# A seventh raw weight tile, and the second tile split first, in an f32 encoder layer on one core

## The chip, the cores and the metric

The kernel runs on 1 core of one Trainium2 chip. The metric is the device time of one execution in microseconds, the median of several runs. The core's engines are TensorE (PE in the profile; PEld is its weight load), VectorE (DVE), ScalarE (ACT), GpSimd (POOL) and SyncE (SP), which issues most DMAs.

## The reference

One pre-norm residual layer over x (256 tokens x 2048 channels, float32), then a final RMSNorm:

```python
h = _rms_norm(x, norm_g)
proj = jnp.einsum('bsd,dn->bsn', h, w_in)        # q k v o za | gates | xb zb | ga gb
ya = _mlstm_branch(q_p, k_p, v_p, o_p, za_p, gif_p, b_if, head_g)
yb = _rglru_branch(xb_p, zb_p, conv_w, conv_b, w_rg, b_rg, lam)
ya = jnp.einsum('bsw,wd->bsd', ya, w_branch_a)
yb = jnp.einsum('bsw,wd->bsd', yb, w_branch_b)
merged = sigmoid(ga_p) * ya + sigmoid(gb_p) * yb
return x + jnp.einsum('bsd,de->bse', merged, w_out)
```

The projections and the three output matrices are matrix products with K = 2048. They are nearly all of the arithmetic, and each weight is read from HBM once.

## The kernel before

Each matrix product is made with split operands, so that the float32 result keeps its precision: a tile v becomes `hi` (a rounded copy, made by ScalarE) and `lo` = v - hi (a subtraction on VectorE), and a product is three matmuls, a.hi + a.lo + b.hi, where a and b are the halves of the activations (`mm`, L174 to L177). A matmul has 128 x 128 weights and 512 columns.

Weights come as tiles of 128 x 1024 f32 (two K-blocks of 128 by 512 output columns, 512 KB) into six tiles of one tag, `raw`. SyncE issues these loads in program order, and each waits until a raw tile is free, that is, until the last instruction that read the load before in it has ended. Four pairs of tiles `whi`/`wlo` hold the halves.

Weights are used in two ways, both in `pair` (L163), which makes two blocks of 512 output columns at a time:

- `plain` (with `load_chunk`, L122 to L142): one raw tile, one copy (L140), one subtraction (L141), then 4 products, 12 matmuls.
- `products` (L186 to L227), called a group in this document: two raw tiles r1 (L190) and r2 (L191) are combined in Strassen's manner, so that 7 products (21 matmuls) do the work of 8. The two tiles are packed on the host so that halves can be subtracted. VectorE forms four sums of half a tile each, t1 (L199, L200) and t2 (L203, L204); four splits are made (`split`, L180 on ScalarE and L181 on VectorE): half of r1 into `b` (512 columns), t1 into h1/l1, t2 into h2/l2, and all of r2 into h3/l3. The order of the program is: b, two sums, split of t1, two sums, split of t2, split of r2. The products p1, p5, p7, p6 go to four small accumulators `aux`, the other three to the large ones, `acc`, in the order p1 (b), p5 and p7 (h1), p6 and one more (h2), and two (h3).

Which of the eight K pieces of a pair are groups, and at which places they stand, is a list by hand. In the four stages `wb` (branch b), gate b, gate a and `wa` (branch a) there are two pairs each: the first with groups at places 0, 2, 4, 6, the second at 1, 3, 5 (`S_WB` to `L_WA`). In `wo` a pair has groups at 0, 2, 4, 6; in the projections for v, o and z there are one or two groups in a pair. After the last group, `aux` is folded into the output by VectorE (L252 to L256), and at the end of a block the large accumulator is added (L262).

The order of instructions on each engine is not the program's. The build places them by a timeline model, with priorities: loads, splits and sums stand in `urgent()` blocks, where earlier program text comes first. The order is then fixed, and each engine takes its instructions one after the other. So in the trace products of a group and plain products are mixed, and a group's `b` can stand on TensorE ahead of products of the group before.

Two other places are touched. `load_chunk` and `products` take their raw tiles from the pool directly (L124, L189). Eight small tiles of 48 columns (`cat` to `spl`, L450), used for the gates near the start (`g_nat`, `g_cum`), lie in the pool of constants; other scratch of that time, the masks among it, lies in a region called E (`et`), which later becomes `hs`, the output of the recurrence.

Of the kernel before, what the change touches and what calls it, by code (L numbers as in the profile page):

```python
# [9 lines left out]
F32 = mybir.dt.float32  # L10
# [5 lines left out]
P = 128  # L16
# [3 lines left out]
NB = 512  # L20
KC = 2
# [8 lines left out]
S_WO = (0, 1, 2, 4)  # L30
L_WB, L_GB, L_GA, L_WA = [((0, 2, 4, 6), (1, 3, 5))] * 4
L_WO = (0, 2, 4, 6)
H_FORMS = (4, 0)
PLAN = (dict(Y=('c0', '', '', 'c1',),
             V=('', '', 'c2 c3', 'g0', '', '', 'g1', '', '', '', 'g2 g3',),
# [11 lines left out]
def f(ap):  # L47
    return ap.bitcast(F32)
# [3 lines left out]
def hybrid_encoder(ctx: ExitStack, tc: tile.TileContext, x, xt, pk, bif, fg, wg, wi, wr, wa, wb, wo, out):  # L52
    nc = tc.nc
    pe, act, dve, pool, sp = nc.tensor, nc.scalar, nc.vector, nc.gpsimd, nc.sync
# [3 lines left out]
    wp = ctx.enter_context(tc.tile_pool(name="wp", bufs=1))  # L58
# [6 lines left out]
    def name(n):  # L65
        uid[0] += 1
        return f"{n}_{uid[0]}"

    def ct(shape, n, dt=F32):
        return cst.tile(shape, dt, tag=n, name=n)  # L70

    def sl(tag, dt=F32, cols=4096):
        return slot.tile([P, cols], dt, tag=tag, name=name("s" + tag))
# [13 lines left out]
    def urgent():  # L87
        uid[0] += 1
        return tc.high_priority(offset=HP - 30 * uid[0])
# [28 lines left out]
        lanes.clear()  # L118

    first_dma = [None]  # L120

    def load_chunk(src, dst=None, tag="w", bufs=4, parts=1, between=()):  # L122
        with urgent():
            raw = wp.tile([P, KC * NB], F32, tag="raw", name=name("raw"), bufs=6)  # L124
            if dst is None:
                hi = wp.tile([P, KC * NB], F32R, tag=tag + "hi", name=name(tag + "hi"), bufs=bufs)
                lo = wp.tile([P, KC * NB], F32R, tag=tag + "lo", name=name(tag + "lo"), bufs=bufs)
            else:
                hi, lo = dst
            w = KC * NB // parts  # L130
            for i in range(parts):
                r = slice(i * w, (i + 1) * w)
                last_dma[0] = (act if between and i == 0 else sp).dma_start(raw[:, r], src[:, r]).ins
                if i == 0:
                    first_dma[0] = last_dma[0]
            for i in range(parts):
                r = slice(i * w, (i + 1) * w)
                if i < len(between):
                    between[i]()
                last_copy[0] = act.copy(hi[:, r], raw[:, r]).ins  # L140
                last_sub[0] = dve.tensor_sub(lo[:, r], raw[:, r], f(hi[:, r])).ins  # L141
        return hi, lo  # L142
# [17 lines left out]
    def four(v):  # L160
        return v.rearrange("p (a b) -> p a b", b=S)

    def pair(src, xhi, xlo, forms, kqs, dst, b11, epilogue, sums=None, places=None, calm=False):  # L163
        aps = []
        accs = [acc_pair()[1] for _ in range(2)]
        banks = [[v[:, :NB], v[:, NB:]] for v in accs]
# [6 lines left out]
        def mm(ps, a, b, wh, wl, stop):  # L173
            pe.matmul(ps, a, wh, start=id(ps) not in began, stop=False)  # L174
            began.add(id(ps))
            pe.matmul(ps, a, wl, start=False, stop=False)  # L176
            pe.matmul(ps, b, wh, start=False, stop=stop)  # L177

        def split(hi, lo, v):
            act.copy(hi, v)  # L180
            dve.tensor_sub(lo, v, f(hi))  # L181

        def wpair():
            return [wp.tile([P, KC * NB], F32R, tag=t, name=name(t), bufs=4) for t in ("whi", "wlo")]

        def products(kq, last):  # L186
            lf, rt_ = slice(0, NB), slice(NB, 2 * NB)
            with urgent():
                r1, r2 = [wp.tile([P, KC * NB], F32, tag="raw", name=name("raw"), bufs=6) for _ in range(2)]  # L189
                sp.dma_start(r1, src[0][kq])  # L190
                sp.dma_start(r2, src[1][kq])  # L191
                bh, bl = b11()
                split(bh, bl, r1[:, lf])
                if sums:
                    t1, t2 = sums()
                else:
                    t1, t2 = [four(hp.tile([P, 2 * NB], F32, tag=t, name=name("t"))) for t in ("vhi", "vlo")]
                v1, v2 = four(r1), four(r2)
                dve.tensor_sub(t1[:, :2], v1[:, 2:], v1[:, :2])  # L199
                dve.tensor_sub(t1[:, 2:], v2[:, :2], v1[:, 2:])  # L200
                h1, l1 = wpair()
                split(four(h1), four(l1), t1)
                dve.tensor_add(t2[:, :2], t1[:, 2:], v1[:, :2])  # L203
                dve.tensor_sub(t2[:, 2:], v2[:, 2:], t2[:, :2])  # L204
                h2, l2 = wpair()
                split(four(h2), four(l2), t2)
                h3, l3 = wpair()
                split(h3, l3, r2)
            fm = forms[kq]

            def xb(kk, tb):
                o = (kq * KC + kk) * S + tb * P
                return xhi(o, o + P), xlo(o, o + P)

            def sf(i):
                return [v[:, i * P:(i + 1) * P] for v in fm]

            if not aps:
                aps.extend(aux(i) for i in range(4))
            p1, p5, p7, p6 = aps  # L220
            mm(p1, *xb(0, 0), bh, bl, last)
            mm(p5, *sf(0), h1[:, lf], l1[:, lf], last)
            mm(p7, *sf(2), h1[:, rt_], l1[:, rt_], last)
            mm(p6, *sf(1), h2[:, lf], l2[:, lf], last)
            mm(banks[0][1], *xb(1, 1), h2[:, rt_], l2[:, rt_], False)
            mm(banks[0][0], *xb(1, 0), h3[:, rt_], l3[:, rt_], False)
            mm(banks[1][0], *sf(3), h3[:, lf], l3[:, lf], False)  # L227

        def plain(kq, jj):
            hi, lo = load_chunk(src[jj][kq])  # L230
# [170 lines left out]
    def et(shape):  # L401
        n = int(np.prod(shape[1:]))
        o = eoff[0]
        eoff[0] += n
        v = est[:shape[0], o:o + n]
        if len(shape) == 3:
            v = v.rearrange("p (a b) -> p a b", b=shape[2])
        return v
# [38 lines left out]
        pool.memset(t, 0.0)  # L447
    gn = ct([P, 2, 16], "gn")
    NS = 48
    cat, ab, ey, sv, qv, pv, ng, spl = (ct([P, NS], n) for n in ("cat", "ab", "ey", "sv", "qv", "pv", "ng", "spl"))  # L450
    c8, c4 = ct([P, 32], "c8"), ct([P, 32], "c4")
    an = et([P, 2, P])
    negM, em = ct([P, 2, 8], "negM"), ct([P, 2, 8], "em")
# [352 lines left out]
    def values(h):  # L806
        if h == 0:
            yas["h"], yas["l"] = sl("A", F32R), sl("B", F32R)
            hf.update({kq: halves(sl(f"F{kq}", F32R, 1024), 0) for kq in H_FORMS})
            for i, kq in enumerate(H_FORMS):  # L810
                rg["work"][f"y{i}"] = lambda kq=kq: forms_h(kq)
# [124 lines left out]
    def b11():  # L936
        nb11[0] += 1
        v = hp.tile([P, 2 * NB], F32R, tag=("to", "zz")[nb11[0] % 2], name=name("b11"))
        return v[:, :NB], v[:, NB:]
# [17 lines left out]
    for p in range(2):  # L957
# [5 lines left out]
        pair((wi[BLK_GA + 2 * p], wi[BLK_GA + 2 * p + 1]), hhi, hlo, forms("h"), S_GA[p], ga[2 * p:], b11, epi_ga, None, L_GA[p])  # L963
    for kq, slot_ in zip(k_ya[2:], H_FORMS[::-1]):
        fslot["a", kq] = halves(sl(f"F{slot_}", F32R, 1024), 0)
# [64 lines left out]

    pair((wo[0], wo[1]), mh, ml, mf_, S_WO, dst, b11, epi_wo, None, L_WO)

# [7 lines left out]
    for tb, a, b, col in ((0, 0, NB, 3), (1, 0, S, 3), (1, S, NB, 4)):  # L1040
        ps = aux()[:, :b - a]
        for k in range(KT):
# [4 lines left out]
            xa, xb = mh(o, o + P), ml(o, o + P)  # L1047
# [79 lines left out]
```

## Time and profile before

| | |
|---|---|
| median of 3 runs | 1028.58 us (1027.71 to 1029.91) |
| the profiled execution, its own time | 1029.06 us |
| its span, first to last instruction | 1027.3 us |
| mean granted TensorE clock | 0.995 |
| instructions | 13760 |
| raw weight loads by SyncE | 358, nearly all of 512 KB |
| HBM read | 196.33 MB, 193 GB/s over the span |

The 358 loads are the rows "raw<-wi" (254), "raw<-wb", "raw<-wa" and "raw<-wo" (32 each) and "raw<-wr" (8) of the profile's last part. Times are in microseconds from the first instruction unless marked ns. A line such as "PE aux L174 <- ACT b L180: 7.6, 4, 3.3" says that TensorE, before writing `aux` at line 174, waited for ScalarE writing `b` at line 180, 7.6 us in total, 4 times, 3.3 us at the longest. In a timeline a row has start, length, engine, line, operation, output and inputs, how many were merged, and in brackets the idle time before it and what ended it. Matmuls overlap in the records (0.39 us long): the distance of two starts is what one costs.

### The profile page before, as it was taken

How to read it: one execution, taken by the hardware profiler on the slowest of the kernel's cores; microseconds unless marked ns; L12 is line 12 of the kernel's file. 1: busy time of each engine (PE TensorE's matmuls, PEld its weight loads, DVE VectorE, ACT ScalarE, POOL GpSimd, SP SyncE). 2: the span in 40 equal slices, each digit the busy share in tenths (PEclk: the TensorE clock that was granted, in tenths of full speed). 3: DMA queues.
4: the chain of work that ended last, by engine and by line, in shares of the span. 5: the costliest groups of instructions: out<-in, count | busy, mean ns of one | idle time of the engine just before them, and what ended most of it. 6: DMA issues, size and time to landing. Idle time of an engine off the chain costs nothing.

```text
span 1027.3 us, 13760 instructions
## 1 busy us (share of the span) xinstructions
PE 1009.0 (98%) x5033; PEld 852.2 (83%) x5033; DVE 896.8 (87%) x1208; ACT 633.6 (62%) x836; POOL 19.5 (2%) x37
## 2 busy tenths in 40 slices
PE   9999999999999999999999998998999999999997
PEld 9888988888888888888888886877888788778886
DVE  6787898889769879996786898999998989999996
ACT  7546477757795776677755554545655556454562
POOL 1000000001001000100100000000000000000000
PEclk9999999999999999999999999999999999999999
DMA  9665555565665566656476465556555565567562
GB/s 349 255 207 167 160 160 190 182 204 166 197 192 164 188 198 194 198 166 212 134 227 189 156 204 187 181 166 228 183 182 207 185 205 207 175 241 282 178 209 82
DMA packets 56387, 199.32 MB, mean 194 GB/s; under 512 B 6400, under 2 KB 7424, under 8 KB 55936
## 3 DMA queue, kind: packets, MB, share of 16 engines
q1 hardware_dynamic: 55456, 197.13, 58.0%
q10 hardware_dynamic: 864, 1.32, 0.4%
q8 instruction: 39, 0.64, 0.3%
q14 instruction: 28, 0.23, 0.1%
HBM read 196.33 MB, written 2.10 MB: 193 GB/s over the span
## 4 chain that ended last, share of the span: by engine, by line
PE 79%; DVE 10%; DMA 6%; issue 3%; ACT 2%; ACTq 0%; DVEq 0%; SPq 0%
PE acc L315 16%; PE acc L176 12%; PE acc L174 12%; PE acc L177 12%; PE acc L318 8%; DMA raw<-wi 4%; DVE wlo L141 3%; PE aux L176 2%; PE aux L174 2%; PE aux L177 2%; DVE wlo L181 2%; DMA raw<-wb 1%; ACT whi L140 1%; PE aux L855 1%; PE aux L721 1%
## 5 line engine op out<-in xcount | busy, mean ns | idle before, releaser
L141 DVE TENSOR_TENSOR wlo<-raw,whi 128x1024 fp32r<-128x1024 f32 (+1 forms) x276 | 332.4, 1212 | 71.8 <-ACT whi L140 70.2
L140 ACT CAST whi<-raw 128x1024 fp32r<-128x1024 f32 (+1 forms) x276 | 285.1, 1045 | 164.5 <-PE acc L177 75.0
L176 PE MATMUL acc<-wlo,sHL 128*128 128x512 f32 x542 | 211.9, 391 | 0.0
L177 PE MATMUL acc<-whi,sHL 128*128 128x512 f32 x542 | 211.2, 390 | 0.0
L174 PE MATMUL acc<-whi,sHL 128*128 128x512 f32 x542 | 208.2, 390 | 0.0
L315 PE MATMUL acc<-sHL,whi 128*128 128x512 f32 x704 | 175.9, 393 | 0.0
L315 PEld LDWEIGHTS acc<-sHL,whi 128*128 128x128 f32 x704 | 127.4, 189 | 23.5
L180 ACT CAST whi<-t 128x1024 fp32r<-128x1024 f32 x78 | 82.0, 1052 | 65.6 <-PE acc L177 28.4
L176 PEld LDWEIGHTS acc<-wlo,sHL 128*128 128x128 f32 x542 | 101.9, 188 | 22.0 <-DVE wlo L141 0.9
L174 PEld LDWEIGHTS acc<-whi,sHL 128*128 128x128 f32 x542 | 101.9, 188 | 21.3 <-DVE xp L330 0.4
L177 PEld LDWEIGHTS acc<-whi,sHL 128*128 128x128 f32 x542 | 101.9, 188 | 20.5
L318 PEld LDWEIGHTS acc<-sHL,wlo 128*128 128x128 f32 x704 | 95.3, 190 | 6.0
L181 DVE TENSOR_TENSOR wlo<-t,whi 128x1024 fp32r<-128x1024 f32 x78 | 94.9, 1219 | 6.1 <-ACT whi L180 5.9
L318 PE MATMUL acc<-sHL,wlo 128*128 128x256 f32 x704 | 99.0, 283 | 0.0
L180 ACT CAST b<-raw 128x512 fp32r<-128x512 f32 x32 | 19.8, 621 | 62.6 <-DMA raw<-wi 33.4
L180 ACT CAST whi<-raw 128x1024 fp32r<-128x1024 f32 x41 | 43.1, 1050 | 19.9 <-PE acc L177 9.1
L181 DVE TENSOR_TENSOR wlo<-raw,whi 128x1024 fp32r<-128x1024 f32 x41 | 50.0, 1219 | 3.6 <-ACT whi L180 3.6
L199 DVE TENSOR_TENSOR t<-raw 128x512 f32<-128x512 f32 x37 | 25.4, 687 | 10.3 <-DMA raw<-wi 4.9
L176 PE MATMUL acc<-wlo,sA 128*128 128x512 f32 x86 | 33.8, 393 | 0.0
L176 PE MATMUL acc<-wlo,sC 128*128 128x512 f32 x86 | 33.8, 393 | 0.0
L177 PE MATMUL acc<-whi,sD 128*128 128x512 f32 x86 | 33.7, 392 | 0.0
L177 PE MATMUL acc<-whi,sB 128*128 128x512 f32 x86 | 33.6, 391 | 0.0
(363 smaller groups left out, 1649.7 us busy)
## 6 DMA issues: line engine op xcount, KB each, us to landing
raw<-wi SPq DMA_DIRECT2D x254, 512.0 KB, 4.1
raw<-wb SPq DMA_DIRECT2D x32, 512.0 KB, 4.2
raw<-wa SPq DMA_DIRECT2D x32, 512.0 KB, 4.3
raw<-wo SPq DMA_DIRECT2D x32, 512.0 KB, 4.6
raw<-wr SPq DMA_DIRECT2D x8, 512.0 KB, 3.9
sB<-x SPq DMA_DIRECT2D x4, 512.0 KB, 7.9
sA<-x SPq DMA_DIRECT2D x1, 2048.0 KB, 9.6
sA<-xt SPq DMA_DIRECT2D x7, 256.0 KB, 6.6
```

The source lines that it names most:

```text
L140: last_copy[0] = act.copy(hi[:, r], raw[:, r]).ins
L141: last_sub[0] = dve.tensor_sub(lo[:, r], raw[:, r], f(hi[:, r])).ins
L174: pe.matmul(ps, a, wh, start=id(ps) not in began, stop=False)
L176: pe.matmul(ps, a, wl, start=False, stop=False)
L177: pe.matmul(ps, b, wh, start=False, stop=stop)
L180: act.copy(hi, v)
L181: dve.tensor_sub(lo, v, f(hi))
L199: dve.tensor_sub(t1[:, :2], v1[:, 2:], v1[:, :2])
L315: pe.matmul(ps[m], hi[:, o:o + P], hl_t[:, 2 * k * S:2 * (k + 1) * S], start=(k == 0), stop=(turn and k == KT - 1), skip_group_check=True)
L318: pe.matmul(ps[m][:, :S], lo[:, o:o + P], hhi(k * S, (k + 1) * S), start=False, stop=(not turn and k == KT - 1), skip_group_check=True)
L721: pe.matmul(dst, wlo[:, o:o + P], xh[:, r], start=False, stop=True)
L855: pe.matmul(num, a, b, start=(n == 0), stop=(n == 5))
```

## The change

```diff
+RAW = 7
...
+    spare, turns = [], [0]
+
+    def raw_tile():
+        i = turns[0] % (RAW + len(spare))
+        turns[0] += 1
+        if i < RAW:
+            return wp.tile([P, KC * NB], F32, tag="raw", name=name("raw"), bufs=RAW)
+        return sl(spare[i - RAW], F32, KC * NB)
...
-            raw = wp.tile([P, KC * NB], F32, tag="raw", name=name("raw"), bufs=6)
+            raw = raw_tile()
...
-                r1, r2 = [wp.tile([P, KC * NB], F32, tag="raw", name=name("raw"), bufs=6) for _ in range(2)]
+                r1, r2 = raw_tile(), raw_tile()
...
                 v1, v2 = four(r1), four(r2)
+                h3, l3 = wpair()
+                split(h3, l3, r2)
                 dve.tensor_sub(t1[:, :2], v1[:, 2:], v1[:, :2])
                 dve.tensor_sub(t1[:, 2:], v2[:, :2], v1[:, 2:])
+                dve.tensor_sub(t2[:, :2], v2[:, :2], t1[:, :2])
+                dve.tensor_sub(t2[:, 2:], v2[:, 2:], t2[:, :2])
                 h1, l1 = wpair()
                 split(four(h1), four(l1), t1)
-                dve.tensor_add(t2[:, :2], t1[:, 2:], v1[:, :2])
-                dve.tensor_sub(t2[:, 2:], v2[:, 2:], t2[:, :2])
                 h2, l2 = wpair()
                 split(four(h2), four(l2), t2)
-                h3, l3 = wpair()
-                split(h3, l3, r2)
...
             mm(p1, *xb(0, 0), bh, bl, last)
+            mm(banks[0][0], *xb(1, 0), h3[:, rt_], l3[:, rt_], False)
             mm(p5, *sf(0), h1[:, lf], l1[:, lf], last)
             mm(p7, *sf(2), h1[:, rt_], l1[:, rt_], last)
+            mm(banks[1][0], *sf(3), h3[:, lf], l3[:, lf], False)
             mm(p6, *sf(1), h2[:, lf], l2[:, lf], last)
             mm(banks[0][1], *xb(1, 1), h2[:, rt_], l2[:, rt_], False)
-            mm(banks[0][0], *xb(1, 0), h3[:, rt_], l3[:, rt_], False)
-            mm(banks[1][0], *sf(3), h3[:, lf], l3[:, lf], False)
...
-    cat, ab, ey, sv, qv, pv, ng, spl = (ct([P, NS], n) for n in ("cat", "ab", "ey", "sv", "qv", "pv", "ng", "spl"))
+    cat, ab, ey, sv, qv, pv, ng, spl = (et([P, NS]) for _ in range(8))
```

The tag `raw` has seven tiles instead of six; the list `spare` stays empty, so `raw_tile` only hands out these seven. In a group, the whole of r2 is split right after `b`, then the four sums are formed one after the other, then t1 and t2 are split. The third sum is now r2's left half minus the first sum, where it was the second sum plus r1's left half: the same value up to rounding, from other operands, so that r1 is read for the last time by the second sum. The seven products follow the order in which their operands are made: b, one of r2, two of t1, one of r2, two of t2. The eight small tiles move from the pool of constants into region E; a raw tile takes 4096 bytes in each partition, the eight small ones 8 x 48 x 4 = 1536.

## The prediction

> **What bounds the kernel now.** I read the busy times first, then the table of windows cut where the rows change character.
>
> ```profile
> span 1027.3 us, 13760 instructions
> PE 1009.0 (98%) x5033; PEld 852.2 (83%) x5033; DVE 896.8 (87%) x1208; ACT 633.6 (62%) x836; POOL 19.5 (2%) x37
> 0.00:583.00 583.00, 581.48 (x3121) 502.11 (x3122) 487.50 (x692) 389.49 (x556) 19.50 (x37) 1.00 0.60 194
> 583.00:1000.00 417.00, 407.19 (x1787) 331.72 (x1786) 390.75 (x481) 236.52 (x264) 0.00 (x0) 0.99 0.59 202
> 672.00:719.00 47.00, 43.02 (x185) 34.06 (x184) 44.09 (x56) 24.33 (x28) 0.00 (x0) 1.00 0.56 191
> ```
>
> The columns of a window are its length, then busy time of PE, PEld, DVE, ACT and POOL, the granted clock, the DMA share and GB/s. Until 583 us TensorE idles 583.00 - 581.48 = 1.5 us: that part is bound by TensorE, and no load can come too early to help it. From 583 to 1000 us (the output halves of `wb`, the two gates, `wa`, `wo`) TensorE idles 417.00 - 407.19 = 9.8 us, while VectorE is 390.75 / 417 = 94% busy. The change removes no TensorE work, so these 9.8 us and what hangs on them are all it can win. Next, who ended TensorE's waits (total us, times, longest), and the stall they come from.
>
> ```profile
> PE aux L174 <- ACT b L180: 7.6, 4, 3.3
> PE aux L174 <- ACT whi L180: 1.1, 2, 0.7
> PE aux L176 <- DVE wlo L181: 0.7, 2, 0.4
> ...
> 625.59 0.39 PE L177 MATMUL acc<-whi,sD 128*128 128x512 f32 x1
> 625.82 0.39 PE L174 MATMUL aux<-whi,sPT 128*128 128x512 f32 x1
> 629.49 0.50 PE L174 MATMUL aux<-b,sC 128*128 128x512 f32 x1 [3.29 <-ACT b L180]
> 630.07 0.39 PE L176 MATMUL aux<-wlo,sPT 128*128 128x512 f32 x1
> 630.85 0.63 PE L177 MATMUL aux<-whi,sPT 128*128 128x512 f32 x1
> 633.41 0.63 PE L177 MATMUL acc<-whi,sD 128*128 128x512 f32 x1
> ...
> 718.76 0.50 PE L174 MATMUL aux<-b,sHL 128*128 128x512 f32 x1 [2.57 <-ACT b L180]
> 721.84 0.63 PE L174 MATMUL aux<-whi,sF 128*128 128x512 f32 x1
> ...
> 804.93 0.50 PE L174 MATMUL aux<-b,sHL 128*128 128x512 f32 x1 [0.95 <-ACT b L180]
> 805.88 0.50 PE L174 MATMUL aux<-whi,sF 128*128 128x512 f32 x1 [0.45 <-ACT whi L180]
> 806.45 0.39 PE L177 MATMUL aux<-whi,sF 128*128 128x512 f32 x1
> ...
> 889.05 0.50 PE L174 MATMUL aux<-b,sA 128*128 128x512 f32 x1 [0.79 <-ACT b L180]
> ```
>
> Four waits for `b` (the split half of a group's first weight tile) make 3.29 + 2.57 + 0.95 + 0.79 = 7.6 us. Each stands once in a stage, as its second pair starts. A matmul normally starts 625.82 - 625.59 = 0.23 us after the one before; so three, a product, take 0.68 us. After the two long stalls TensorE runs slowly: from 630.85 to 633.41 lie six starts, 0.43 us each, 0.2 us too much; some eight matmuls are in that state after each stall (the 0.63 us ones), which makes 2 x 8 x 0.2 = 3.2 us more. After the 0.95 us it does not happen (0.39 at 806.45). All that can be won is thus about 9.8 + 3.2 = 13 us.
>
> Why is `b` late? The first stall, on three engines: SyncE's issues, VectorE, ScalarE.
>
> ```profile
> 610.07 1.53 SPq L133 DMA_DIRECT2D raw<-wb  x2
> 612.41 0.33 SPq L190 DMA_DIRECT2D raw<-wb  x1
> 616.57 0.33 SPq L191 DMA_DIRECT2D raw<-wb  x1
> 620.68 2.06 SPq L133 DMA_DIRECT2D raw<-wb  x2
> 624.15 0.33 SPq L190 DMA_DIRECT2D raw<-wb  x1
> ...
> 615.32 1.22 DVE L181 TENSOR_TENSOR wlo<-raw,whi 128x1024 fp32r<-128x1024 f32 x1
> 617.89 0.69 DVE L199 TENSOR_TENSOR t<-raw 128x512 f32<-128x512 f32 x1 [1.35 <-DMA raw<-wb]
> 621.17 1.22 DVE L141 TENSOR_TENSOR wlo<-raw,whi 128x1024 fp32r<-128x1024 f32 x1
> 622.90 1.22 DVE L141 TENSOR_TENSOR wlo<-raw,whi 128x1024 fp32r<-128x1024 f32 x1
> 627.57 1.21 DVE L181 TENSOR_TENSOR wlo<-t,whi 128x1024 fp32r<-128x1024 f32 x1
> ...
> 617.82 0.62 ACT L180 CAST b<-raw 128x512 fp32r<-128x512 f32 x1 [2.24 <-DMA raw<-wb]
> 618.34 3.90 ACT L140 CAST whi<-raw 128x1024 fp32r<-128x1024 f32 x4
> 628.82 0.62 ACT L180 CAST b<-raw 128x512 fp32r<-128x512 f32 x1 [4.20 <-DMA raw<-wb]
> ```
>
> Every issue leaves as VectorE lets go of a raw tile: 616.57 follows the split of the last group's second tile (615.32 + 1.22 = 616.54), the load of the late `b` at 624.15 follows a plain split (622.90 + 1.22 = 624.12). It lands 4.65 us on, when ScalarE can copy it (628.82). So the ring of six raw tiles is full, and the second tile, split last in its group, holds the queue from 612.41 to 616.57, with all that SyncE issues behind it.
>
> **The change part by part.** *The seventh tile.* Each issue needs one release fewer, so it leaves when the issue before it leaves now: the next group's first tile 612.41 - 611.27 = 1.14 us earlier (the second of the two issues at 610.07 begins at 610.07 + 1.53 - 0.33 = 611.27), its second tile 616.57 - 612.41 = 4.16 us earlier, the late one at the release of 621.17 + 1.22 = 622.39 in place of 624.15, 1.76 us earlier. The first shift also takes 1.14 of the 1.35 us that VectorE waited at 617.89 and of the 2.24 us that ScalarE waited before 617.82, with four plain copies queued behind. What is late next is the split of the group's first sums (627.57 + 1.21 = 628.78), for which the low-part matmul of 630.07 waits: shifted by 1.14 us it ends at 627.64. TensorE is free at 625.82 + 0.23 = 626.05 and has the two matmuls that need only high parts, 0.45 us, so about 1.15 us of idle stay: 3.29 - 1.15 = 2.1 us won. The second stall has the same sequence; I give it the same share, 2.57 x 2.1 / 3.29 = 1.6 us. The third (0.95 for `b` and 0.45 for the sums' copy) I let lose 1.0 us, the fourth, 0.79 us and shorter than the 1.76 us shift, all of it; the waits on sums elsewhere, (1.1 - 0.45) + 0.7 = 1.35 us, lose 0.4 us. Sum 2.1 + 1.6 + 1.0 + 0.8 + 0.4 = 5.9 us. The two long stalls fall to about 1 us, near the 0.95 us that left the clock alone, so the 3.2 us of slow matmuls go too: 9.1 us.
>
> The Trainium skill ("TensorE: Matmul & The Clock Gate", Part 1, the two states) has the clock halve after an idle window of about 3.4 us. The rows do not agree: 2.57 us was enough. By the page's figure as a threshold neither stall would cost any slow matmul, and the win would be the 5.9 us alone.
>
> *The order on VectorE and ScalarE.* No instruction is added or removed: an addition becomes a subtraction of the same shape, and the group keeps four sums and four splits.
>
> ```profile
> L199 DVE TENSOR_TENSOR t<-raw 128x512 f32<-128x512 f32 x37 | 25.4, 687 | 10.3 <-DMA raw<-wi 4.9 <-DMA raw<-wa 2.4 <-DMA raw<-wb 1.3
> L181 DVE TENSOR_TENSOR wlo<-t,whi 128x1024 fp32r<-128x1024 f32 x78 | 94.9, 1219 | 6.1 <-ACT whi L180 5.9
> L200 DVE TENSOR_TENSOR t<-raw,raw 128x512 f32<-128x512 f32 x37 | 25.4, 686 | 4.0 <-DMA raw<-wb 1.9 <-DMA raw<-wa 1.3 <-DMA raw<-wi 0.9
> L262 DVE TENSOR_TENSOR sE<-sE,acc 128x1024 f32<-128x1024 f32 x4 | 4.8, 1215 | 0.0
> ```
>
> With 0.69 us for `b`'s split and each sum and 1.22 us for a full split, VectorE's time in a group is 0.69 + 4 x 0.69 + 3 x 1.22 = 7.1 us either way. Before, operands are ready at 0.7 (`b`, one product), 3.3 (first sums, two), 5.9 (second sums, two) and 7.1 (second tile, two); after, at 0.7 (one), 1.9 (second tile, two), 5.9 (two) and 7.1 (two). At no moment is less supplied, and from 1.9 to 3.3 us 1.36 us of TensorE work more. That moves work forward and adds none, so I book nothing; the cover, if the schedule drops it, is worth at most 1.36 us a stall. The second tile's last reader is then the fourth sum, at 1.9 + 2.8 = 4.7 us instead of 7.1 us: 2.4 us sooner, which is the same queue that the seventh tile already frees, so it is not counted again. Against it, the split of the second tile now stands ahead of the first sum, which needs the first tile alone. If the second tile is late, the sums queue behind it, and the waits that now stand at L200 (4.0 us in the whole kernel) would show there: between 0 and 4.0 us, and I take 0, as that tile's issue is the one that gains 4.16 us. The four sums together need no copy between them; some of the 5.9 us of waits for ScalarE before L181 goes, up to 5.9, taken as 0 because VectorE's waits away from the stalls are cover.
>
> *The order on TensorE.* The same 21 matmuls per group. A product into the first accumulator moves from sixth to second place, one into the other accumulator from seventh to fifth, two products or 1.36 us sooner. Where a pair opens with a group (first pairs of four stages and `wo`) they can meet the previous pair's last addition (L262, 1.22 us). The first accumulator is given up a whole run of plain products before; the second costs between 0 and 5 x 1.36 = 6.8 us. I take 0, as no row shows TensorE's array waiting for L262.
>
> *The eight small tiles* only change place. They enter a region that already holds the masks, read later than they are; the next owner waits for the masks anyway. Zero. *Small new waits*: the whole order of each engine is made anew from a timeline model. The rows before 583 us show what a schedule of this kind leaves, 1.5 us; I put 1 us.
>
> The sum is 9.1 - 1 = 8.1 us on the profiled execution, whose own time is 1029.06 us (span 1027.3 and 1.8 us around it), 0.5 us over the median of 1028.58. Against the median: **1020.5 us**.
>
> **The rivals.** *VectorE bounds these stages.* In the window with the second stall it is 44.09 / 47 = 94% busy. Then `b` comes sooner and TensorE waits for the sums instead, whose split is now 1.22 us later within the group; the 1.36 us put forward are given back at the second sums. Left is a shift of a few tenths at each stall: 1028 us. The 1.35 us wait for a load on a busy VectorE speaks against it. The Trainium skill ("Perfetto Trace Analysis", Identifying the Most-Contended Engine) says to improve the engine with the highest occupancy first, and that for VectorE it is a fair measure; it would have this rival. Its section Optimization Strategy reads repeated equal gaps as too few buffers, and the four alike waits agree with that one.
>
> *All stalls go.* VectorE has 417 - 390.75 = 26.3 us of idle in these stages, twice the 13 us. If the new order uses it, 1028.6 - 13 = 1015.6 us.
>
> *The split pairs are held too long* (slower). There are four `whi`/`wlo` pairs. The pair handed out first in a group is now the second tile's, held until the fifth product instead of the third: 2 x 0.68 = 1.36 us more before a plain chunk can have it. It decides where ScalarE already stands waiting for TensorE to free a `whi` and VectorE has nothing else:
>
> ```profile
> ACT whi L140 <- PE acc L177: 28.3, 19, 3.6
> ```
>
> That is 19 waits from 583 to 1000 us. Reaching TensorE in four of them costs 4 x 1.36 = 5.4 us, with nothing else won 1034 us. For it, the waits are there; against it, they are ScalarE's, and VectorE sat idle for few of them.
>
> *The change does nothing here*, because the schedule keeps its loads where they are: falls in with 1028 us.
>
> **How the numbers follow.** Forecast 0.55; VectorE-bound or nothing 0.18; all stalls gone 0.12; pairs held 0.15. A difference of 0.2%, 2.1 us, is about what a measurement of this kernel can tell from none, so "the same" is 1026.5 to 1030.6. A third of the VectorE case wins a little more than that, 0.06: faster 0.55 + 0.12 + 0.06 = 0.73, same 0.12, slower 0.15. The forecast's own range is 1015.6 to 1025.6 us (from all of the 13 us to half of the 5.9 with the slow matmuls staying, 3 us). For 8 in 10 the lower end takes in most of the case without stalls, 1014, the upper the VectorE case and a small part of the slow one, 1030.5.
>
> **What would show it.** Right: the four waits for `b` total under 3 us, no 0.63 us matmuls near 630 and 720, the second tile's issue a few tenths behind the first's, the L199 waits for loads well under 10.3 us in all, TensorE idle 4 us or less from 583 to 1000. Wrong: the same idle, ended by DVE L181 or ACT whi L180 (VectorE-bound); more waits of ACT whi for PE with VectorE idle behind them (pairs held); new stalls before 583 us, where I expect none.

## The result, and the profile after

The change makes the kernel slower: 1033.71 us in the median of 11 runs (1031.02 to 1038.28) against 1029.53 us (1026.13 to 1032.71, 11 runs) before, a ratio of 1.0045 [1.0026, 1.0065]. The forecast was 1020.5 us, faster, with a range up to 1030.5. The profiled execution took 1035.92 us, its span 1034.2 us. All changed lines lie 9 further down than before: L140 and L141 are now L149 and L150, `mm` is L183 to L186, `split` L189 and L190, the loads of a group L199 and L200, the four sums L210 to L213, the folding L261 to L265, the addition of the large accumulators L271.

The head of the page of the changed kernel:

```profile
span 1034.2 us, 13758 instructions
PE 1010.7 (98%) x5033; PEld 852.5 (82%) x5033; DVE 897.9 (87%) x1208; ACT 640.8 (62%) x840; POOL 18.8 (2%) x37
```

The same number of instructions on TensorE and VectorE and nearly the same busy time; ScalarE has 4 more and 7 us more. Of the 6.9 us by which the span grew, 1.7 us are longer busy time of TensorE and 5.2 us are idle time. The table of windows of the changed kernel, with the columns as before:

```profile
0.00:583.00 583.00, 577.70 (x3100) 497.94 (x3101) 482.90 (x687) 393.94 (x559) 18.79 (x37) 1.00 0.60 195
583.00:1000.00 417.00, 405.82 (x1777) 330.66 (x1776) 392.05 (x481) 237.05 (x263) 0.00 (x0) 0.99 0.61 200
```

TensorE now idles 583.00 - 577.70 = 5.3 us in the first part, where it idled 1.5, and 417.00 - 405.82 = 11.2 us in the second, where it idled 9.8. What TensorE waited for in the changed kernel, the two longest groups after 583 us:

```profile
PE aux L183 <- ACT b L189: 4.4, 3, 1.7
PE aux L183 <- ACT whi L189: 3.3, 5, 1.0
...
PE acc L185 <- DVE wlo L150: 2.4, 2, 1.9
```

The waits for `b` did fall, from 7.6 to 4.4 us, but they stand in the same three places, and others have come beside them. The last line is of the window before 583 us: two new waits for VectorE's split of a plain tile, in the heads (the projections for v, o and z).

**The handover.** But for two waits, of 1.0 us at 684 and 0.3 us at 782 us, all the waits of TensorE after 583 us lie where a stage's second pair starts. There the two large accumulators `acc` change hands: a first product of the second pair may go into them only after VectorE has added them to the first pair's output (L271). In the meantime TensorE has only products into `aux`. The timeline of the changed kernel at gate a, TensorE, VectorE, ScalarE and SyncE:

```profile
807.09 0.39 PE L186 MATMUL acc<-whi,sHL 128*128 128x512 f32 x1
807.32 0.39 PE L183 MATMUL aux<-b,sHL 128*128 128x512 f32 x1
...
808.62 0.94 PE L183 MATMUL aux<-whi,sF 128*128 128x512 f32 x2 [0.46 <-ACT whi L189]
810.20 0.50 PE L185 MATMUL aux<-wlo,sF 128*128 128x512 f32 x1 [0.64 <-DVE wlo L190]
...
812.90 0.65 PE L183 MATMUL aux<-b,sHL 128*128 128x512 f32 x1 [1.51 <-ACT b L189]
813.34 0.63 PE L183 MATMUL acc<-whi,sHL 128*128 128x512 f32 x1
...
806.60 1.21 DVE L190 TENSOR_TENSOR wlo<-raw,whi 128x1024 fp32r<-128x1024 f32 x1
807.73 0.68 DVE L264 TENSOR_TENSOR sC<-aux,sC 128x512 f32<-128x512 f32 x1
808.33 0.68 DVE L265 TENSOR_TENSOR sC<-aux,sC 128x512 f32<-128x512 f32 x1
808.93 1.21 DVE L190 TENSOR_TENSOR wlo<-t,whi 128x1024 fp32r<-128x1024 f32 x1
810.06 2.34 DVE L271 TENSOR_TENSOR sC<-sC,acc 128x1024 f32<-128x1024 f32 x2
...
812.23 0.62 ACT L189 CAST b<-raw 128x512 fp32r<-128x512 f32 x1 [3.66 <-DMA raw<-wi]
...
807.84 0.33 SPq L199 DMA_DIRECT2D raw<-wi  x1
```

The last product into the old accumulators starts at 807.09, the first into the new ones at 813.34: 6.25 us, in which TensorE starts ten matmuls into `aux`. At 0.23 us each, these and the last old one take 2.5 us and leave 3.7 us of idle time. Two things fill it. VectorE has the split of the second tile, two foldings and the split of the first sums (808.93) ahead of the additions, which start only at 810.06. And TensorE has the product of the stage's seventh and last `b` (812.90) in its queue ahead of the first product into `acc`, though an accumulator is free from about 810.06 + 1.21 = 811.3: that `b` waits for a load that left at 807.84, as a raw tile came free. The matmuls behind it take 0.63 us: from 812.9 to 816.4 us the granted clock is 0.53.

The same place in the kernel before, TensorE's last old and first new product and VectorE's additions:

```profile
802.61 0.39 PE L177 MATMUL acc<-whi,sHL 128*128 128x512 f32 x1
807.14 0.40 PE L174 MATMUL acc<-whi,sHL 128*128 128x512 f32 x1
...
805.07 2.35 DVE L262 TENSOR_TENSOR sC<-sC,acc 128x1024 f32<-128x1024 f32 x2
```

These are 4.53 us with eight matmuls into `aux` between, so 2.5 us of idle time, and no matmul is slow.

The same handover in the kernel with the seventh tile and the new order on VectorE but TensorE's old order (e3_vector_order below, the same line numbers):

```profile
799.41 0.39 PE L186 MATMUL acc<-whi,sHL 128*128 128x512 f32 x1
799.64 0.39 PE L183 MATMUL aux<-b,sHL 128*128 128x512 f32 x1
...
800.94 0.73 PE L183 MATMUL aux<-whi,sF 128*128 128x512 f32 x2 [0.46 <-ACT whi L189]
802.00 0.50 PE L183 MATMUL acc<-whi,sHL 128*128 128x512 f32 x1 [0.33 <-DVE sC L271]
...
809.16 0.39 PE L183 MATMUL aux<-b,sHL 128*128 128x512 f32 x1
...
799.60 1.21 DVE L190 TENSOR_TENSOR wlo<-raw,whi 128x1024 fp32r<-128x1024 f32 x1
800.73 2.34 DVE L271 TENSOR_TENSOR sC<-sC,acc 128x1024 f32<-128x1024 f32 x2
803.00 1.22 DVE L190 TENSOR_TENSOR wlo<-t,whi 128x1024 fp32r<-128x1024 f32 x1
...
805.02 0.62 ACT L189 CAST b<-raw 128x512 fp32r<-128x512 f32 x1 [0.85 <-DMA raw<-wi]
```

Here the additions stand ahead of the split of the sums. From 799.41 to 802.00 are 2.59 us with five matmuls into `aux` between; with the last old one that is 1.4 us, so 1.2 us are idle. The seventh group's `b` is copied only at 805.02, after the handover as well, and costs nothing: its product stands at 809.16, behind the products into `acc`.

**The heads.** The other new stall, 3.7 us at 326 to 335 us (distances of starts, less the usual ones), begins up to 40 us earlier on ScalarE. Its timeline in the changed kernel, the function of each line being L732 sigmoid, L735 tanh, L753 exponential, L758 root:

```profile
286.33 1.28 ACT L753 ACT_TABLE_LOAD   x1
287.63 1.71 ACT L753 ACTIVATE sC<-sC,c 128x256 f32<-128x256 f32 x4
289.24 1.99 ACT L149 CAST whi<-raw 128x1024 fp32r<-128x1024 f32 x2
291.24 1.28 ACT L732 ACT_TABLE_LOAD   x1
292.54 0.84 ACT L732 ACTIVATE sC<-aux,pks 128x256 f32<-128x256 f32 x2
...
331.99 0.50 PE L185 MATMUL acc<-wlo,sHL 128*128 128x512 f32 x1 [1.95 <-DVE wlo L150]
```

In the kernel before, all exponentials come after the last sigmoid, with one load, and both roots after the last exponential, with one more:

```profile
290.73 1.28 ACT L744 ACT_TABLE_LOAD   x1
292.02 1.71 ACT L744 ACTIVATE sC<-sC,c 128x256 f32<-128x256 f32 x4
...
294.57 1.71 ACT L744 ACTIVATE sC<-sC,c 128x256 f32<-128x256 f32 x4
296.28 1.28 ACT L749 ACT_TABLE_LOAD   x1
```

In the changed kernel four exponentials stand ahead of a last sigmoid, so that the tables are loaded again for it (291.24) and for the other exponentials; one exponential stands between the two roots, with two more loads. In all the page counts 840 ScalarE instructions instead of 836: 4 more loads of 1.28 us, 5.1 us. The scans that use the results start 4.9 us later on VectorE (319.34 instead of 314.47), and with them come the splits for which TensorE waits at 331.99.

**The whole span.** The distance of two starts, less the usual distance for the shape, is what TensorE loses, by waiting or by a slow clock. Summed over the profiled executions this is 23.7 us before and 30.5 after, which accounts for the whole difference of the spans: 5.8 and 9.6 us up to 583 us, 13.7 and 17.8 us around the four handovers (610 to 642, 703 to 732, 790 to 819 and 875 to 900 us), 4.1 and 3.1 us elsewhere.

### The profile page after: what moved, and what is told of

The parts are those of the page before. It is cut to its first block, busy times and chain, and to the rows that moved or that the text cites. A ratio compares the mean times of both kernels' runs of the same rounds, so it can differ in the third digit from the quotient of the medians.

```text
span 1034.2 us, 13758 instructions
## 1 busy us (share of the span) xinstructions
PE 1010.7 (98%) x5033; PEld 852.5 (82%) x5033; DVE 897.9 (87%) x1208; ACT 640.8 (62%) x840; POOL 18.8 (2%) x37
## 4 chain that ended last, share of the span: by engine, by line
PE 84%; DVE 8%; DMA 4%; issue 2%; ACT 1%; DVEq 0%; SPq 0%; ACTq 0%
PE acc L324 15%; PE acc L185 14%; PE acc L183 14%; PE acc L186 14%; PE acc L327 8%; PE aux L183 3%; PE aux L186 3%; PE aux L185 3%; DMA raw<-wi 2%; DVE wlo L150 2%; DVE wlo L190 2%; PE aux L864 1%; DMA raw<-wb 1%; PE aux L730 1%; PE aux L729 1%
## 5 line engine op out<-in xcount | busy, mean ns | idle before, releaser
L149 ACT CAST whi<-raw 128x1024 fp32r<-128x1024 f32 (+1 forms) x276 | 286.3, 1044 | 180.1 <-PE acc L186 97.9
L150 DVE TENSOR_TENSOR wlo<-raw,whi 128x1024 fp32r<-128x1024 f32 (+1 forms) x276 | 331.4, 1210 | 74.6 <-ACT whi L149 73.0
L186 PE MATMUL acc<-whi,sHL 128*128 128x512 f32 x542 | 212.1, 391 | 0.0
L183 PE MATMUL acc<-whi,sHL 128*128 128x512 f32 x542 | 210.0, 392 | 0.9 <-DVE xp L339 0.5
L189 ACT CAST whi<-t 128x1024 fp32r<-128x1024 f32 x78 | 81.8, 1051 | 63.8 <-PE acc L186 31.0
L183 PEld LDWEIGHTS acc<-whi,sHL 128*128 128x128 f32 x542 | 102.5, 189 | 22.6 <-DVE xp L339 1.0
L186 PEld LDWEIGHTS acc<-whi,sHL 128*128 128x128 f32 x542 | 102.5, 189 | 20.7
L190 DVE TENSOR_TENSOR wlo<-t,whi 128x1024 fp32r<-128x1024 f32 x78 | 94.8, 1218 | 7.2 <-ACT whi L189 6.7
L190 DVE TENSOR_TENSOR wlo<-raw,whi 128x1024 fp32r<-128x1024 f32 x41 | 49.9, 1217 | 3.0 <-ACT whi L189 3.0
L189 ACT CAST whi<-raw 128x1024 fp32r<-128x1024 f32 x41 | 43.1, 1050 | 7.7 <-PE acc L186 3.6
L189 ACT CAST b<-raw 128x512 fp32r<-128x512 f32 x32 | 19.8, 621 | 40.8 <-DMA raw<-wi 22.0
L186 PE MATMUL acc<-whi,sD 128*128 128x512 f32 x86 | 33.9, 395 | 0.0
L183 PE MATMUL acc<-whi,sA 128*128 128x512 f32 x86 | 33.3, 393 | 0.4 <-DVE sD L271 0.4
L186 PE MATMUL acc<-whi,sB 128*128 128x512 f32 x86 | 33.6, 390 | 0.0
```

## Experiments

Every kernel was timed beside the kernel before, in four sets (e1 to e4, e5 to e8, e9 to e12, e13 to e16), each on another chip; the medians of the kernel before were 1029.57, 1029.37, 1029.43 and 1028.99 us, and the ratios are against these runs. "V" is the new order on VectorE and ScalarE, "T" the new order of the products on TensorE.

**The three parts taken apart.** e1 has seven tiles and both old orders, e2 both new orders and six tiles, e3 seven tiles and V alone, e4 seven tiles and T alone. All have the moved small tiles. The edits, from the changed kernel:

```diff
e1: V and T as before;  e3: T as before;  e4: V as before
...
e2:
-RAW = 7
+RAW = 6
```

> Seventh raw tile, with both orders (VectorE's and TensorE's) as before the change. Theory H (held pairs): the loss comes from splitting the second tile first, because its whi/wlo pair is taken before that of the sums and then stands blocked while the large accumulators change hands at the start of a second pair; so the ring alone must not lose: 1024 to 1029 us, and the waits for b at the four second pairs shrink from 7.6 us. Rival R (the ring itself costs: more loads in flight, another schedule): about 1033 us as with the whole change. Rival V (VectorE bounds these stages): 1028 to 1030 us, the stalls as long as before with another releaser.

> Both new orders with six raw tiles. Theory H: slower than before by as much as the whole change or more, 1033 to 1038 us, since the early split stays and the earlier loads are gone. Rival R: 1029 us, as before. Rival V: 1028 to 1031 us.

> Seven raw tiles, VectorE's new order (second tile split first, four sums together), TensorE's products in the order of before. Theory H: the loss is on this side, 1032 to 1036 us, and the waits on whi of the first sums stay at the second pairs. A rival P, by which TensorE's order is at fault (products into the large accumulators moved ahead), expects 1025 to 1029 us.

> Seven raw tiles, VectorE's order of before, TensorE's products in the new order. Theory H: as with the ring alone within 2 us. Rival P: 1032 to 1036 us, because the two products of the second tile, whose split comes last here, stand ahead of others.

Measured: e1 1025.58 us, 0.9961 [0.9947, 0.9976]; e2 1036.22 us, 1.0070 [1.0049, 1.0090]; e3 1023.64 us, 0.9945 [0.9924, 0.9966]; e4 1024.21 us, 0.9950 [0.9934, 0.9967]. All four theories fail as stated; H has the numbers of e1, e2 and e4 right and fails at e3, the run that was to show its mechanism. The seventh tile gains 3.9 us by itself. With it, each new order alone is no loss (2.0 and 1.4 us faster again, about what the intervals can tell), and only the two together lose 8 us. The profile of e2 has its losses at other places than that of the whole change: against the kernel before, TensorE loses 7.2 us more up to 583 us (27 table loads, and waits of 1.88 us at 188 and 2.97 us at 512 us) and 0.7 us less around the handovers. The kernel with the early split and its long-held pair is among the fastest.

**Where the two orders lose.** e5 uses V and T only in the five late stages, e6 only in the heads (v, o, z); the other groups keep the old orders. e7 is e3 with six tiles. e8 exchanges two products of the whole change, to see whether its loss hangs on one accidental schedule.

```diff
e5: both orders under "if forms is not hf:", else the old ones
e6: both orders under "if forms is hf:", else the old ones
e7: e3 with RAW = 6
e8:
-            mm(p5, *sf(0), h1[:, lf], l1[:, lf], last)
             mm(p7, *sf(2), h1[:, rt_], l1[:, rt_], last)
+            mm(p5, *sf(0), h1[:, lf], l1[:, lf], last)
```

> Seven raw tiles; the two new orders only in the four stages wb, gate b, gate a, wa and in wo, the orders of before in the projections for v, o and z. In the whole change ScalarE loads its activation table 25 times, before 21; the four more (5.1 us of ScalarE) stand between 286 and 308 us, and TensorE stalls 3.7 us at 326 to 335 us behind them. Theory T (table loads: the two new orders together let the build put exponentials between sigmoids in the projections): 21 loads, no stall at 326, and 1028 to 1030 us. If the loss lies in the late stages (their boundaries between pairs): 1032 to 1034 us.

> Seven raw tiles; the two new orders only in the projections for v, o and z, the orders of before in the late stages. Theory T: 25 table loads, the stall of about 3.7 us near 326 us, and 1029 to 1031 us, that is 4 to 5 us over the ring alone (1025.6). If the loss lies in the late stages: 1025 to 1026 us, as the ring alone.

> Six raw tiles, VectorE's new order, TensorE's order of before. With seven tiles this made 1023.6 us against 1025.6 for the ring alone. If the seventh tile is worth some 4 us whatever the order: 1027 to 1029 us. If VectorE's order needs the seventh tile: 1030 us or more.

> The whole change with p7 ahead of p5, two products of one operand that become ready together: an edit that should cost nothing, to see what a mere shuffle of the schedule does. If the build's order is robust: 1033 to 1035 us. If the loss is an accident of the schedule: any value from 1024 to 1040 us.

Measured: e5 1031.47 us, 1.0028 [1.0013, 1.0042]; e6 1027.01 us, 0.9972 [0.9958, 0.9987]; e7 1027.19 us, 0.9977 [0.9960, 0.9993]; e8 1034.01 us, 1.0042 [1.0027, 1.0056]. Against e1, the late stages lose 5.9 us and the heads 1.4 us; the sum is near the 8.1 us of the whole. e6 has the 3.7 us stall at 326 to 335 us of the whole change, e5 does not; both times lie between the ranges that were expected. In its profile e6 wins back about as much at other places, the larger part from 345 to 583 us and around the first two handovers. e8 shows that the loss doesn't hang on the order of these two products. From e7, V gains 2 us with six tiles too.

**The order of the handover.** e9 is the whole change, and VectorE may split the first sums of a second pair's first group only after the two additions. e10 does this to e3, e11 to the kernel before, e12 to e1. No wait on data is taken away; only the order on VectorE is given. The condition in the edit also holds for one pair in the heads (o and z of the second head), which gets the order too.

```diff
-                split(four(h1), four(l1), t1)
+                act.copy(four(h1), t1)
+                if places[0] == 1 and kq == kqs[0]:
+                    with tc.issue_after(last_add[0]):
+                        dve.tensor_sub(four(l1), t1, f(four(h1)))
+                else:
+                    dve.tensor_sub(four(l1), t1, f(four(h1)))
...
-                dve.tensor_add(dst[jj], dst[jj], accs[jj])
+                last_add[0] = dve.tensor_add(dst[jj], dst[jj], accs[jj]).ins
```

> The whole change with one added order: at the first group of a second pair, VectorE splits the first sums only after the two additions that empty the first pair's accumulators. Theory F (form of the handover): at the starts of wb's, gate b's and gate a's second pair the whole change has the sums' split (and so the four low-part products and the fifth group's b product on TensorE) ahead of these additions, and stalls of 5.8, 5.4 and 5.2 us; the kernel with the vector order alone has the additions first at both gates, and 1.4 and 1.3 us there. With the additions first at all three, 16.4 us of stall become about 4.2, so 1033.7 - 12.2 = 1021.5 us, no half-clock matmuls at 640, 725 and 814, and the 3.7 us at 326 to 335 us stay. Rival L (the late load): what ends the wait is the b of the next or the fifth group, which waits for a raw tile; the addition only moves it, and the time stays at 1031 to 1034 us with the b ending the same waits a few products later. Rival V (VectorE has no room): what is put off is missed later, the time falls by half at most, 1027 us or more.

> The same added order on seven tiles with the new VectorE order and the old TensorE order, which has the additions behind the sums' split at wb alone. Theory F: its 5.7 us at 627 to 638 us fall to about 1.4, the gates do not change, 1023.6 - 4.3 = 1019.3 us. Rivals L and V: 1022.5 us or more.

> The same added order on the kernel before (six tiles, both old orders), which also has the additions behind the split of the sums at wb and gate b. Theory F alone: its stalls of 5.3, 4.4 and 2.5 us at these three places fall to about 1.4 each, 1029.4 - 8 = 1021.4 us: most of what the prediction hoped for, with nothing of the change. Rival L (late load): with six tiles the third group's b still comes 3.3 and 2.6 us late and the stalls keep that, so they fall by 2 us each at most and the time to 1025 us or stays at 1029.

> The same added order on seven tiles with both old orders, whose stalls were 5.6 us at wb and 5.2 us at gate b, and none at gate a. Theory F: both fall to about 1.4 us, 1025.6 - 8 = 1017.6 us, the fastest of all here. Rivals L and V: 1023 us or more. Against e11: under F and L the seventh tile is worth the same 3 to 4 us with the order as without it.

Measured: e9 1029.99 us, 1.0004 [0.9991, 1.0016]; e10 1022.99 us, 0.9938 [0.9919, 0.9958]; e11 1030.15 us, 1.0034 [1.0011, 1.0057]; e12 1023.79 us, 0.9947 [0.9927, 0.9967]. So the order is worth 3.7 us in the whole change, and at most 2 us in e10 and e12. In e11 it gains nothing: the late `b` still makes TensorE wait 2.3 us each at `wb` and gate b, and while its handovers shrink (table below), TensorE loses 7.5 us after 583 us outside them, where it lost 4.1. Theory F was right in its place and much too large in its size; the ranges of rival V held in the three kernels for which they were given. The timeline of e9 at gate b, VectorE, shows why (the split is L191 here, the last two foldings L270 and L271, the additions L277):

```profile
715.51 0.69 DVE L191 TENSOR_TENSOR b<-raw,b 128x512 fp32r<-128x512 f32 x1 [0.74 <-ACT b L190]
716.46 1.23 DVE L191 TENSOR_TENSOR wlo<-raw,whi 128x1024 fp32r<-128x1024 f32 x1 [0.25 <-ACT whi L190]
717.60 0.68 DVE L270 TENSOR_TENSOR sD<-aux,sD 128x512 f32<-128x512 f32 x1
718.20 0.68 DVE L271 TENSOR_TENSOR sD<-aux,sD 128x512 f32<-128x512 f32 x1
718.99 2.35 DVE L277 TENSOR_TENSOR sD<-sD,acc 128x1024 f32<-128x1024 f32 x2
```

The last old product starts at 715.20. The sums' split is gone from in front of the additions, but `b`, the second tile's split and two foldings are still there, 3.8 us from 715.20 to 718.99, with VectorE waiting for `b`'s load among them. (The late `b` that e9's expectation gives to the fifth group is the seventh of its stage, by the count of the loads.)

The idle time of TensorE at the four handovers, worked out from the timelines as above (from the last old to the first new product, less 0.23 us for the last old matmul and for every one between; the slow matmuls that can follow are not in it), in us:

| kernel | wb | gate b | gate a | wa | sum | time |
|---|---|---|---|---|---|---|
| before | 4.4 | 4.2 | 2.5 | 1.2 | 12.2 | 1029.5 |
| after | 4.5 | 4.3 | 3.7 | 1.2 | 13.7 | 1033.7 |
| e1, seven tiles alone | 3.8 | 4.4 | 0 | 0 | 8.2 | 1025.6 |
| e3, with V | 4.0 | 1.3 | 1.2 | 1.1 | 7.6 | 1023.6 |
| e4, with T | 3.7 | 1.5 | 0.3 | 0 | 5.4 | 1024.2 |
| e5, V and T late | 3.9 | 3.5 | 3.8 | 1.2 | 12.4 | 1031.5 |
| e9, after + handover | 2.6 | 3.7 | 1.7 | 1.5 | 9.5 | 1030.0 |
| e10, e3 + handover | 2.1 | 1.7 | 1.9 | 1.1 | 6.8 | 1023.0 |
| e11, before + handover | 3.2 | 3.2 | 3.0 | 1.4 | 10.7 | 1030.2 |
| e12, e1 + handover | 2.6 | 3.0 | 0.3 | 0 | 5.8 | 1023.8 |
| e14, e4 + handover | 1.5 | 1.2 | 0.3 | 0 | 2.9 | 1022.3 |

These sums alone don't order the times: e2 has 12.1 us, as the kernel before, and takes 1036.2 us.

**The rest of the loss, and the missing combination.** e13 is e9 with an order in the heads: no exponential before the last tanh, no root before the last exponential. e16 has this order and not the handover's. e14 is e4 with the handover's order, e15 is e4 with six tiles.

```diff
             st["a"] = act.activation(tv[d][:, r], av[d][:, r], AF.Tanh, ...).ins
+            st.setdefault("t", []).append(st["a"])
...
-            with tc.issue_after(st["a"]), tc.issue_after(last_copy[0]):
+            with ExitStack() as order, tc.issue_after(last_copy[0]):
+                for t in st["t"]:
+                    order.enter_context(tc.issue_after(t))
...
+                    st.setdefault("e", []).append(i.ins)
...
-            with tc.issue_after(st["a"]), tc.issue_after(last_copy[0]):
+            with ExitStack() as order, tc.issue_after(st["a"]), tc.issue_after(last_copy[0]):
+                for e in st["e"]:
+                    order.enter_context(tc.issue_after(e))
```

> The whole change with two added orders: the accumulators' additions ahead of the sums' split (as in e9_handover), and in the heads no exponential before the last tanh and no root before the last exponential, which takes ScalarE's table loads from 25 back to 21. Theory S (the loss is a sum of places, one in the heads and the handovers): the 3.7 us at 326 to 335 us go, so 1030.0 - 3.7 = 1026.3 us. Rival O (the two orders together are slow by themselves, wherever the idle time shows): the 3.7 us come up elsewhere, 1029 us or more.

> The whole change with the order in the heads alone (21 table loads); every handover stays as the change has it. Theory S: 1033.7 - 3.7 = 1030.0 us, stalls of 5 to 6 us at all three handovers as before. Rival O: 1032 us or more. Rival M (the table loads of 1.28 us in the heads are hidden; the 1.4 us between the heads' and the ring's kernels was all there is): 1032.3 us.

> Seven tiles, the old VectorE order, the new TensorE order, and the additions ahead of the sums' split. The kernel without the addition has 5.3 us at wb between the last old product and the first addition, 2.8 us at gate b and nothing at gate a. Theory S: wb falls to about 2.9 us, as in the other kernels that got this order, 1024.2 - 2.4 = 1021.8 us. Rival: as with the ring alone, gate b takes it back, 1023 to 1024 us.

> Six tiles, the old VectorE order, the new TensorE order: the one combination of the three parts that has not run. If the new TensorE order is worth with six tiles what it is with seven (1.4 us), 1028.1 us; the seventh tile is then worth 3.9 us under it. If the new TensorE order needs the seventh tile, 1029.5 us or more.

Measured: e13 1026.73 us, 0.9974 [0.9963, 0.9985]; e16 1029.66 us, 0.9990 [0.9975, 1.0006]; e14 1022.29 us, 0.9933 [0.9918, 0.9948]; e15 1034.92 us, 1.0061 [1.0040, 1.0082]. Theory S holds in all its three numbers (1026.3, 1030.0 and, for e14, 1021.8). For e15 the second reading holds, that T needs the seventh tile, with a loss well beyond the 1029.5 us named for it. ScalarE in e13 at the same place:

```profile
288.71 0.55 ACT L741 ACTIVATE sD<-sC,c 128x256 f32<-128x256 f32 x1
289.28 1.28 ACT L762 ACT_TABLE_LOAD   x1
290.58 0.91 ACT L762 ACTIVATE sC<-sC,c 128x256 f32<-128x256 f32 x2
...
294.08 1.70 ACT L762 ACTIVATE sC<-sC,c 128x256 f32<-128x256 f32 x4
295.79 1.28 ACT L770 ACT_TABLE_LOAD   x1
```

One load for the exponentials (L762 here), one for the roots (L770), 21 in the kernel as before; TensorE has no wait from 322 to 340 us. In e14 the handover at gate b, VectorE and TensorE (L277 adds the accumulators, L215 splits the first sums):

```profile
714.85 0.68 DVE L191 TENSOR_TENSOR b<-raw,b 128x512 fp32r<-128x512 f32 x1
715.45 2.34 DVE L277 TENSOR_TENSOR sD<-sD,acc 128x1024 f32<-128x1024 f32 x2
717.72 1.21 DVE L215 TENSOR_TENSOR wlo<-t,whi 128x1024 fp32r<-128x1024 f32 x1
...
716.72 0.50 PE L184 MATMUL acc<-whi,sHL 128*128 128x512 f32 x1
```

The first new product starts 716.72 - 713.89 = 2.8 us after the last old one (713.89, six matmuls between), 1.2 us of them idle, and no matmul after it is slow. e14 has the lowest median of all, 6.7 us below the kernel before; the ratios of e10, e3 and e12 lie within its interval, that of e4 (0.9950) just outside. The medians of the eight combinations, in us:

| tiles | old orders | V | T | V and T |
|---|---|---|---|---|
| six | 1029.5 | 1027.2 | 1034.9 | 1036.2 |
| seven | 1025.6 | 1023.6 | 1024.2 | 1033.7 |

## Why the prediction was wrong

**What held.** The loads were late for the reason given, and the seventh tile brings them forward: in e1 TensorE's waits for `b` after 583 us are 1.2 us instead of 7.6. The tile gains with every order, 2.5 to 3.9 us and 10.7 us under T. The moved small tiles, booked at zero, come with the seventh tile in e1; no run shows their share alone. One row named to show a right forecast, the first sum's wait for loads, did fall, from 10.3 us to 6.1 in e1 and 1.6 in the whole change (L210), where the second tile's split now stands ahead of that sum. The others did not come: the waits for `b` are 4.4 us instead of under 3, matmuls of 0.63 us stand behind all three of them, and TensorE idles 11.2 us after 583 us instead of 4 or less.

**The size of that gain.** Forecast were 5.9 us of waits and 3.2 us of slow matmuls; e1 gains 3.9 us in all. The step that failed is "What is late next": it named the sums' split, with 1.15 us of idle left. Next are the additions that free the accumulators. In e1 the two long handovers stay at 3.8 and 4.4 us though the waits for `b` in them are down to 0.24 and 0.95 us; its two longest waits are both for L271, 1.7 us each. The late `b` was one of several waits in one gap, and 2.1 of its 3.29 us were booked as if the gap would shrink with it. Forecast were 2.1 and 1.6 us at `wb` and gate b, 1.0 and 0.8 at gate a and `wa`; the idle time of the four handovers fell by 0.6, -0.3, 2.5 and 1.2 us, so that the sum came nearer than its terms did. The slow matmuls, 3.2 us for two stalls, went at gate b in e1 and stayed at `wb`, with both gaps about as long as before. The prediction looked at the accumulators only for the start of a stage (L262, "between 0 and 5 x 1.36 = 6.8 us") and took 0, where the place to look was the second pair inside a stage.

**"That moves work forward and adds none, so I book nothing"**, for V. Alone it is even a small gain (e3, e7). **"I take 0"**, for T, with 6.8 us as the other end. Alone with seven tiles it is a small gain (e4); with six tiles it costs 5.9 us (e15), and on top of V 9 to 10 us (e2 against e7, the whole change against e3). The failed step is that these terms were added as if independent. Each was costed on one group's supply and demand, but it is the build that lays out VectorE, and with both orders it puts 3.8 and 3.0 us between the last old product and the additions at gate b and gate a, against 1.4 and 1.3 us in e3. Set against e1, which has its additions even later at `wb` and gate b, the handover that both orders spoil is that of gate a: no idle time there in e1, 3.7 us in the whole change.

**"New stalls before 583 us, where I expect none"**, and 1 us for small waits. The heads got 3.7 us. ScalarE's activation functions are in no line of the diff, yet the new layout interleaved them. Putting them back (e16) takes 4.0 us off the whole change, more than the 1.4 us by which e6 differs from e1.

**The ledger.** Of the 8.1 us by which the change stands above its seventh tile alone, the order of the handover carries 3.7 (e9) and the order in the heads 3.3 (e13 against e9); 1.1 us are left in e13. These two were shown by experiment: each order was put right by itself, and the time came down.

**The rivals.** The slower rival, split pairs held too long, named a time of 1034 us; that this is near the one measured is luck, as its mechanism is not what the runs show. It was to show in ScalarE's waits for a free `whi` tile, and these did grow (L149 behind TensorE's `acc`, 28.3 us before, 49.1 after). But they are 43.2 us in e1 and 49.0 in e4, with the old split, and 43.8 in e3, with the early one and among the lowest times. The VectorE-bound rival came nearer the place: TensorE waits for VectorE at the handover, with the sums' split as one of the pieces. It missed the sign, since it only let the gain vanish. The Trainium skill ("Perfetto Trace Analysis", Identifying the Most-Contended Engine) takes occupancy as a fair measure for VectorE, though not for TensorE, and would optimize the engine with the highest first. The windows agree in part: TensorE, at 97%, idles where VectorE, at 94% on average, has a backlog of 3 to 4 us.

**What stays open.** Why the build's model ranks the instructions so under both orders, and not under one, was not tried; only that their place costs the time. Why T costs 5.9 us with six tiles is open too: the profiled execution of e15, at 1030.67 us, is the shortest of its runs (up to 1038.75). The others have a lower granted clock, down to 0.991 against 0.999, but no trace shows which waits led to it. Runs of the changed kernel differ in the same way, 1031.0 us twice at 0.999 and 1038.3 at 0.990. This isn't what separates the kernels: at 0.999, e1 has a run of 1023.3 us and e14 has three of 1020.8 to 1023.5.

## What to carry to other kernels

Where accumulators pass from one block of work to the next, write down what each engine has queued between the last old product and the first new one; a wait that ends such a gap can be removed with the gap left standing. When a build lays out the instructions anew, the edit's own rows don't bound its cost: look for what else will be placed differently, on engines that the diff doesn't touch too. Take a change of several parts apart before keeping or dropping it: here three of the parts' combinations gain 4 to 6 us, and all together lose 4.

## What was not expected of the hardware

The clock halved after a gap with no long idle stretch in it: at gate a in the changed kernel the waits are 0.46, 0.64 and 1.51 us within 6.25 us, 3.7 us of idle time by the starts, and the next matmuls take 0.63 us. The idle time of a gap does not decide it alone: such matmuls follow 2.0 us at gate b in e7 and 2.1 us at `wb` in e10, and none follow 4.4 us at gate b in e1 or 3.7 us at `wb` in e4. The Trainium skill ("TensorE: Matmul & The Clock Gate", Part 1) gives one idle window of about 3.4 us; the rows differ from that as a condition on a single stretch.

A table load stands in the rows with 1.28 us, and the next activation starts 292.54 - 291.24 = 1.30 us after it. The Trainium skill ("ScalarE: Activation LUTs", What ACT_TABLE_LOAD costs) has the same 1283 ns and a drain of about 1380 ns beside it; no such drain is seen here, where the copies end at 289.24 + 1.99 = 291.23 us and the load starts at 291.24.
